# When the attention's parts run: one block per four chain steps, or evenly over the first 56 of 64

## The chip, the cores and the metric

The kernel runs on one core of a Trainium2 chip. The metric is the device time of one execution in microseconds (us). The kernel before took 3438.3 us (median of three runs, 3437.28 to 3444.45).

## The reference, cut to what matters

One encoder layer over 2048 tokens of width 1024. After a normalisation, one projection gives the inputs of two token mixers and their gates. A router then sends tokens to 16 experts of a SwiGLU block, which is more than half of the time but is not touched here.

```
u = rms_norm(x) @ w_in
# mixer 1, RWKV-7: state S (64x64 per head, 8 heads), one scan forward, one in reverse
S = S*w_t - (S@kk_t)(a_t*kk_t)' + v_t k_t' ;  y_t = S @ r_t
y_rwkv = (layer_norm(y_forward + y_reverse)*ln_w + ln_b + bonus) * g
# mixer 2, attention in a window of 128 tokens to each side: 16 blocks of 128 queries
y_attn = softmax(q k' + alibi, sink) v
merged = sigmoid(g1)*(y_rwkv @ w_pr) + sigmoid(g2)*(y_attn @ w_pa)
x = x + merged @ w_out ;  x = x + moe(rms_norm(x)) ;  out = rms_norm(x)
```

## The kernel before

The program has these stages: the projections; a preparation of the scans; the chains (in `token_mixers`, from about 970 to 1760 us); the merge of the mixers (`stage3`); the experts (`stage4`).

**The chains.** Each scan is cut into 64 chunks of 32 tokens. A step s works on chunk s of the forward scan and on chunk 63-s of the reverse scan. In a step, and for each scan, TensorE multiplies (L654), ScalarE copies (`ur`, L658), TensorE multiplies (L661), ScalarE copies four quarters into the tile `W` (L666), TensorE multiplies (L672) and VectorE writes the new state into the `W` of the next step (L675). Each waits for the one before it. The eight small matmuls of L679 read the same `W` and give the step's output `y`; the chain does not wait for them at once. Four steps make a group, and a group fills one `y` tile in PSUM for each scan. There is one such tile per scan (`ps_y`, one buffer).

**What ties the groups together.** A `W` tile (`W_8640` and `W_8641` of the forward scan, `W_8662` and `W_8663` of the other) serves two steps, and there are two per scan. So the `W` of a group's first two steps is loaded anew for the first two steps of the next group: four DMAs of 32 KB on the SP queue (L622, issued with one for `PRA`, L611), which wait until the L679 of the old group have read it. From the second half on (group 8 and later) VectorE adds `y` to the stored half of the other scan (`yacc`, L841, two buffers). That frees the `y` tile for the next group. Then `finish_rwkv` runs twice per group, once for each of two token blocks: layer norm on VectorE, four transposes on TensorE (L705) into a `pa` tile, `yt` on ScalarE (L709, four activations), L711 and L712 on VectorE, and a DMA of `yt` to `yr` (L713). `yt` and its second input `bgl` (L689) have one buffer each:

```
yt = k.ln.tile([128, NPAIR, 128], F32, name="yt")      # pool k.ln has bufs=1
k.ps_a = es.enter_context(tc.tile_pool(name="ps_a", bufs=3, space=PSUM))
```

**Work beside the chains.** `gates.run(7)` puts 7 matmuls (L495) of the remaining projections behind each scan's step. The attention is a generator per block of 128 queries: loads; scores of 8 heads (L748 and L749, each pair followed by L751 on VectorE) in four parts; transposes (L780) and products with the values (L787) in the rest. A middle block has 8 parts, the first and last have 7, so there are 126. `pieces` runs the next parts, 3, 2, 4 and 0 of them behind the four steps of a group, and stops at a block's end: one block per group, the last behind step 62.

**What sets the order.** The program is handed to a scheduler, which orders each engine's instructions by a simulated timeline. Instructions of the chain have priority as if written 1200 instructions earlier, those of `finish_rwkv` 500; all others go by their place in the program. Buffers of a pool are taken in the order of the program: the `pa` tile of a `finish_rwkv` is one of three that the attention's parts before it in the program use too, so its transposes stand behind those parts. `stage3` begins with the matmuls of L86 to L88 into `pm`; its PSUM tiles lie where those of the chains were.

Of the kernel before, what the change touches and what calls it, by code (L numbers as in the profile page):

```python
# [21 lines left out]
NQ = 4  # L22
QT = T // NQ
NBLK = T // 128
# [25 lines left out]
GATE_FIRST, GATE_MID = 24, 40  # L50
GATE_PREP, GATE_STEP = 5, 7
QKV = 20, 19, 15, 16, 17, 18
PIECES = 3, 2, 4, 0
LEAD = 1200


# [478 lines left out]
def mixers(k):  # L535
    nc, tc = k.nc, k.tc
    with ExitStack() as es:
# [37 lines left out]
        k.inv = es.enter_context(tc.tile_pool(name="inv", bufs=1))  # L575
        k.gc = k.inv.tile([128, 2, NPAIR, T // C], F32, name="gc")
        token_mixers(k, gates, el)


# [266 lines left out]
def token_mixers(k, gates, el):  # L846
# [4 lines left out]
    with ExitStack() as es:  # L851
# [96 lines left out]
        def invert(n):  # L948
            if late:
                late[0].run(n)  # L950
                if late[0].i > C:
                    late.pop(0)
# [11 lines left out]
            nc.vector.tensor_copy(k.abias[:, i], t)  # L964
        att = [attention(k, b) for b in range(NBLK)]

        def pieces(n):
            for _ in range(n):
                if att:
                    gates.need(min(NQ - 1, (NBLK - len(att) + 1) // 4))  # L970
                if att and next(att[0], 0) == 0:
                    att.pop(0)
                    break

        def between(mark):
            gates.run(GATE_STEP, after=mark)

        gates.run(GATE_MID)
        for s in range(NSTEP):
            run.step(s, between)  # L980
            pieces(PIECES[s % 4])
            invert(4)
        while att:
            pieces(9)
        while gates.todo:
            gates.run(24)

# [550 lines left out]
```

## Time and profile before

| | us |
|---|---|
| median of three runs | 3438.3 |
| the profiled execution's own time | 3432.75 |
| span of the profile, first to last instruction | 3430.9 |
| last TensorE instruction of the chains, end | 1761.1 |
| first TensorE instruction of `stage3` | 1805.4 |

The profile names engines PE (TensorE matmul), PEld (its weight load), DVE (VectorE), ACT (ScalarE), POOL (GpSimd) and SP (the queue that issues most DMAs). L495 is line 495 of the kernel. A row of a timeline has start, duration, engine, line, operation, tiles, and, in brackets, the idle time before it and what ended that. One row of L654, L661, L672 or L679 in the order below is two matmuls in the trace (x8 there, x16 here), and so is one of L787.

### The profile page before, as it was taken

To read this page: it belongs to the slowest core of one execution; us is meant where nothing else is said; L and a number is where in the kernel's file an instruction comes from. 1 tells how busy PE (TensorE), PEld (TensorE's weight loads), DVE (VectorE), ACT (ScalarE), POOL (GpSimd) and SP (SyncE) were. 2 spreads that over 40 slices of the span, in tenths; PEclk is the share of its full clock that TensorE was granted. 3 is DMA by queue.
4 is the path that set the end of the run, shared out by engine and by line. 5 is a ranking of instruction groups with operands and counts; after the bars stand their busy time and mean duration, and the time that the engine had idled before them with its cause. 6 is when DMAs were issued, how large, how long until landed. Compare 5 with 4: busy or idle time off the path is not lost. (4 is left out here: it accounts for less than half of the span.)

```text
span 3430.9 us, 65672 instructions
## 1 busy us (share of the span) xinstructions
PE 3170.0 (92%) x26062; PEld 2603.2 (76%) x26062; DVE 2321.3 (68%) x4902; ACT 1470.2 (43%) x2828; POOL 285.5 (8%) x457
## 2 busy tenths in 40 slices
PE   7999898889779998999969999659999999999998
PEld 6888676677556655666647888559999999999997
DVE  6434679898968889666776666466666666666665
ACT  5111455545424545455553333314444444444443
POOL 0000000000021111001000000001111111121111
PEclk9999899999989999999989999879999999999999
DMA  4212587868787777577666554336666666666663
GB/s 145 85 74 89 173 244 226 247 203 253 207 205 191 171 185 168 145 195 186 176 179 222 195 198 168 147 119 242 217 236 236 247 244 224 231 244 243 237 232 124
DMA packets 464579, 665.19 MB, mean 194 GB/s; under 512 B 162312, under 2 KB 345480, under 8 KB 445968
## 3 DMA queue, kind: packets, MB, share of 16 engines
q1 hardware_dynamic: 387824, 535.14, 50.5%
q10 hardware_dynamic: 58304, 59.79, 5.3%
q0 software_dynamic: 18144, 66.07, 5.1%
q8 instruction: 206, 3.38, 0.4%
q14 instruction: 101, 0.83, 0.1%
HBM read 483.66 MB, written 177.21 MB: 193 GB/s over the span
## 5 line engine op out<-in xcount | busy, mean ns | idle before, releaser
L495 PE MATMUL mm<-h,w 128*128 128x512 f32 x2112 | 602.1, 419 | 28.7 <-ACT ev L519 7.5
L86 PE MATMUL pg<-xs,wg 128*128 128x256 f32 x2048 | 583.6, 285 | 0.0
L87 PE MATMUL pg<-xs,wg 128*128 128x256 f32 x2048 | 582.0, 284 | 0.0
L88 PE MATMUL pg<-xs,wg 128*128 128x256 f32 x2048 | 579.6, 283 | 0.0
L495 PEld LDWEIGHTS mm<-h,w 128*128 128x128 f32 x2112 | 383.2, 194 | 123.0 <-DVE w L93 9.8
L87 PEld LDWEIGHTS pg<-xs,wg 128*128 128x128 f32 x2048 | 392.4, 192 | 4.6 <-DVE xs L1244 0.2
L86 PEld LDWEIGHTS pg<-xs,wg 128*128 128x128 f32 x2048 | 392.3, 192 | 4.6 <-ACT xs L1243 0.2
L88 PEld LDWEIGHTS pg<-xs,wg 128*128 128x128 f32 x2048 | 392.4, 192 | 0.0
L93 DVE TENSOR_TENSOR wg<-raw,wg 128x2048 fp32r<-128x2048 f32 x125 | 286.3, 2291 | 106.4 <-ACT wg L92 106.2
L92 ACT ACTIVATE w<-wraw 128x1024 fp32r<-128x1024 f32 x135 | 142.6, 1058 | 309.4 <-issue 155.2
L1331 ACT ACTIVATE sg<-pg 128x256 f32<-128x256 f32 x128 | 49.3, 385 | 488.4 <-PE pg L88 460.0
L92 ACT ACTIVATE wg<-raw 128x2048 fp32r<-128x2048 f32 x125 | 238.7, 1910 | 0.0
L405 DVE TENSOR_TENSOR tmp<-X,N 128x1 f32<-128x1 f32 (+30 forms) x248 | 188.4, 760 | 37.9 <-DMA N<-pra 17.6
L78 PE MATMUL mm<-h,w 128*128 128x512 f32 x480 | 190.0, 397 | 18.5 <-ACT w L92 12.8
L87 PE MATMUL py<-wd,hd 128*128 128x512 f32 x512 | 203.1, 397 | 0.0
L86 PE MATMUL py<-wd,hd 128*128 128x512 f32 x512 | 201.0, 393 | 0.0
L666 ACT ACTIVATE W<-ps 32x128 f32<-32x128 f32 x512 | 137.5, 269 | 147.9 <-PE ps L661 125.3
L93 DVE TENSOR_TENSOR w<-wraw,w 128x1024 fp32r<-128x1024 f32 x135 | 164.8, 1222 | 50.4 <-ACT w L92 50.0
L88 PE MATMUL py<-wd,hd 128*128 128x512 f32 x512 | 198.4, 390 | 0.0
L79 PE MATMUL mm<-h,w 128*128 128x512 f32 x480 | 189.3, 395 | 0.0
L80 PE MATMUL mm<-h,w 128*128 128x512 f32 x480 | 188.8, 394 | 0.0
L1332 DVE TENSOR_TENSOR sg<-pg,sg 128x256 f32<-128x256 f32 x128 | 54.1, 423 | 192.6 <-ACT sg L1331 192.6
(302 smaller groups left out, 6374.0 us busy)
## 6 DMA issues: line engine op xcount, KB each, us to landing
raw<-w_exp SPq DMA_DIRECT2D x128, 1536.0 KB, 6.9
wraw<-w_in SPq DMA_DIRECT2D x103, 512.0 KB, 5.1
PRA<-pra SPq DMA_DIRECT2D x64, 512.0 KB, 5.2
pra<-PR SPq DMA_DIRECT2D x64, 256.0 KB, 4.0
pra<-A SPq DMA_DIRECT2D x64, 256.0 KB, 3.8
kt<-KT ACTq DMA_DIRECT2D x128, 128.0 KB, 5.0
gl<-ev ACTq DMA_DIRECT2D x64, 256.0 KB, 4.2
KT<-kt SPq DMA_DIRECT2D x128, 128.0 KB, 5.3
```

What stands on the lines that cost most here:

```text
L78: nc.tensor.matmul(ps, lhsT=w[:, 0, i], rhs=hs[i][:, 0], start=(i == 0), stop=False)
L79: nc.tensor.matmul(ps, lhsT=w[:, 0, i], rhs=hs[i][:, 1], start=False, stop=False)
L80: nc.tensor.matmul(ps, lhsT=w[:, 1, i], rhs=hs[i][:, 0], start=False, stop=(i == KD - 1))
L86: nc.tensor.matmul(out, lhsT=w[0], rhs=x[0], start=start, stop=False)
L87: nc.tensor.matmul(out, lhsT=w[0], rhs=x[1], start=False, stop=False)
L88: return nc.tensor.matmul(out, lhsT=w[1], rhs=x[0], start=False, stop=stop)
L92: nc.scalar.activation(hi, x, AF.Copy)
L93: (eng or nc.vector).tensor_sub(lo, x, hi)
L405: nc.vector.tensor_mul(tmp[:, :i, :i], X[:, r, r], col[:, None, :].to_broadcast([128, i, i]))
L495: nc.tensor.matmul(self.ps, lhsT=w[:, t // 2, i], rhs=h[:, t % 2], start=(self.i == 0), stop=(self.i == 3 * KD - 1))
L666: nc.scalar.activation(W[qd(u), o, e].rearrange("p g i -> p (g i)"), ps[qd(u), 128:256], AF.Copy)
L1332: nc.vector.tensor_mul(sg, pg[:, 1], sg)
```

## The change

`pieces` with its table of numbers is replaced. Behind step s, parts run while fewer than (128/56)(s+1) have run, so two or three behind each step; the 126th stands behind step 54, and behind the last nine steps stands none. No instruction is added or removed, and the wait for the projections of later token quarters (`gates.need`) is called as before.

```diff
-PIECES = 3, 2, 4, 0
+ATT_END = 56
...
-        def pieces(n):
-            for _ in range(n):
-                if att:
-                    gates.need(min(NQ - 1, (NBLK - len(att) + 1) // 4))
-                if att and next(att[0], 0) == 0:
-                    att.pop(0)
-                    break
+        def piece():
+            gates.need(min(NQ - 1, (NBLK - len(att) + 1) // 4))
+            if next(att[0], 0) == 0:
+                att.pop(0)
...
+        parts = 0
         for s in range(NSTEP):
             run.step(s, between)
-            pieces(PIECES[s % 4])
+            while att and parts * ATT_END < 8 * NBLK * (s + 1):
+                piece()
+                parts += 1
             invert(4)
         while att:
-            pieces(9)
+            piece()
```

What the scheduler makes of it differs from step 26 on. The first place is TensorE at the boundary between group 12 (steps 48 to 51) and group 13. Before, around step 49, the forward scan's L679 on `W_8640` stood between the chain's own matmuls:

```order
L679 MATMUL y_16874<-W_8640,PRA_16498 32x64
L654 MATMUL ps_17110<-W_8662,PRA_16567 32x64 x8
L679 MATMUL y_16874<-W_8640,PRA_16498 32x64 x3
L495 MATMUL mm<-h,w 128x512 x7
L679 MATMUL y_16874<-W_8640,PRA_16498 32x64
L672 MATMUL ps_17060<-W_8640,KT_8644 64x64 x8
L679 MATMUL y_16874<-W_8640,PRA_16498 32x64 x3
```

(`y_16874` and below `y_17136` and `y_17137` are the `y` tiles of group 12; a number on `W_` or `ps_` names one buffer.) The next L654 on `W_8640`, of step 52, stood 52 rows further. Now all 64 L679 of the group stand at its end, and that L654 is the row behind them:

```order
L679 MATMUL y_17136<-W_8640,PRA_16740 32x64 x16
L679 MATMUL y_17136<-W_8641,PRA_17142 32x64 x9
L705 MATMUL pa<-ident,yacc 128x128 x4
L748 MATMUL pa<-kh,qs 128x384
L749 MATMUL pa<-kl,qs 128x384
L679 MATMUL y_17136<-W_8641,PRA_17142 32x64 x5
L748 MATMUL pa<-kh,qs 128x384
L749 MATMUL pa<-kl,qs 128x384
L679 MATMUL y_17136<-W_8641,PRA_17142 32x64 x2
L679 MATMUL y_17137<-W_8662,PRA_16809 32x64 x16
L679 MATMUL y_17137<-W_8663,PRA_17202 32x64 x16
L654 MATMUL ps_17855<-W_8640,PRA_17449 32x64 x8
```

The L679 moved from the steps that compute their `W` to the end of the group; the same holds at the ends of groups 10, 11, 13, 14 and 15.

The second place is TensorE at the end of the chains. Before, eight score pairs (L748, L749) of the last attention block stood behind the last chain matmuls, and behind those came its transposes and products, two `finish_rwkv` and `stage3`:

```order
L780 MATMUL pa<-ident,sc 128x128 x5
L787 MATMUL pa<-pT,vs 64x512
L780 MATMUL pa<-ident,sc 128x128 x11
L705 MATMUL pa<-ident,yacc 128x128 x4
L787 MATMUL pa<-pT,vs 64x512 x2
L705 MATMUL pa<-ident,yacc 128x128 x4
L787 MATMUL pa<-pT,vs 64x512
L86 MATMUL pm<-ysp,w 128x512
```

Now the row of the last chain matmuls (L661) is followed by this:

```order
L661 MATMUL ps_19408<-ur_19417,X 32x64 x8
L705 MATMUL pa<-ident,yacc 128x128 x4
L787 MATMUL pa<-pT,vs 64x512 x2
L705 MATMUL pa<-ident,yacc 128x128 x4
L787 MATMUL pa<-pT,vs 64x512
L679 MATMUL y_19062<-W_8640,PRA_18755 32x64 x16
L679 MATMUL y_19062<-W_8641,PRA_19068 32x64 x16
L679 MATMUL y_19063<-W_8662,PRA_18815 32x64 x16
L679 MATMUL y_19063<-W_8663,PRA_19128 32x64 x16
L705 MATMUL pa<-ident,yacc 128x128 x16
L86 MATMUL pm<-ysp,w 128x512
```

The last block's scores and transposes moved ahead of the chain's end, and behind it now stand six `finish_rwkv` (four L705 each: those of groups 13, 14 and 15) where two stood.

## Rows read from the trace of the kernel before

**Rows 1.** Busy us (and instructions) of each engine by stretch, then PE clock, DMA share, GB/s.
```profile
1280.00:1400.00 120.00, 103.48 (x1491) 68.24 (x1490) 108.20 (x234) 55.09 (x169) 13.30 (x42) 0.91 0.69 175
...
1600.00:1700.00 100.00, 99.78 (x1302) 65.37 (x1301) 72.19 (x223) 58.37 (x174) 9.84 (x32) 1.00 0.67 181
1700.00:1760.00 60.00, 57.85 (x793) 35.68 (x792) 39.64 (x122) 32.90 (x103) 2.44 (x8) 1.00 0.57 150
1761.00:1805.00 44.00, 14.13 (x53) 7.60 (x48) 29.29 (x90) 21.61 (x49) 0.00 (x0) 0.65 0.66 210
```

**Rows 2.** The same view, of L658 alone: two of them make a step.
```profile
1500.00:1600.00 100.00, 4.48 (x17) 0.98 0.75 196
```

**Rows 3.** Timeline of PE at the end of the chains.
```profile
1758.61 0.42 PE L661 MATMUL ps<-ur,X 32*32 32x64 f32 x16
1759.88 1.19 PE L679 MATMUL y<-W,PRA 128*32 128x64 f32 x16 [0.84 <-ACT W L666]
...
1763.29 0.36 PE L748 MATMUL pa<-kh,qs 128*128 128x256 f32 x1 [2.23 <-DVE qs L737]
...
1795.17 0.66 PE L705 MATMUL pa<-ident,yacc 128*128 128x128 f32 x4
1795.76 1.07 PE L787 MATMUL pa<-pT,vs 128*64 128x512 f32 x2
1805.43 0.79 PE L86 MATMUL pm<-ysp,w 128*128 128x512 f32 x1 [8.59 <-ACT yt L709]
```

**Rows 4.** Timeline of ACT at the end of the chains.
```profile
1755.83 1.46 ACT L709 ACTIVATE yt<-pa,vec 128x128 f32<-128x128 f32 x4
...
1759.55 1.15 ACT L666 ACTIVATE W<-ps 32x128 f32<-32x128 f32 x4 [0.60 <-PE ps L661]
...
1765.82 1.50 ACT L709 ACTIVATE yt<-pa,vec 128x128 f32<-128x128 f32 x4 [1.28 <-DMA yr<-yt]
...
1794.27 1.50 ACT L709 ACTIVATE yt<-pa,vec 128x128 f32<-128x128 f32 x4 [1.97 <-PE pa L705]
...
1803.87 1.50 ACT L709 ACTIVATE yt<-pa,vec 128x128 f32<-128x128 f32 x4 [6.40 <-DMA yr<-yt]
```

**Rows 5.** Timeline of PE within a step; the next row's start ends a row's share.
```profile
1632.33 0.43 PE L679 MATMUL y<-W,PRA 128*32 128x64 f32 x16
1632.69 0.69 PE L672 MATMUL ps<-W,KT 128*64 128x64 f32 x16
...
1633.76 0.34 PE L748 MATMUL pa<-kh,qs 128*128 128x384 f32 x1
1633.94 0.33 PE L749 MATMUL pa<-kl,qs 128*128 128x384 f32 x1
...
1634.56 1.91 PE L495 MATMUL mm<-h,w 128*128 128x512 f32 x7
```

**Rows 6.** Who waited for L625 (clearing in `W`), 1400 to 1760 us: us, times.
```profile
PEld ps L654: 0.7, 2
```

**Rows 7.** Timeline of SP: a reload of `W`; the DMAs of a finish.
```profile
1645.13 2.13 SPq L622 DMA_DIRECT2D W<-vtok  x4
...
1797.26 0.57 SPq L689 DMA_DIRECT2D bgl<-bg  x1
1797.88 0.66 SPq L713 DMA_DIRECT2D yr<-yt  x1
```

**Rows 8.** Issue to landing, 1400 us on: `W` (L622), then `yr` (L713).
```profile
DMA to landing us min/median/max: 1.6/3.8/6.8
...
DMA to landing us min/median/max: 2.6/3.9/7.2
```

**Rows 9.** Timeline of DVE behind the L709 of 1794.27.
```profile
1795.81 0.69 DVE L711 TENSOR_TENSOR yt<-yt,bgl 128x512 f32<-128x512 f32 x1 [1.09 <-ACT yt L709]
1796.54 0.69 DVE L712 TENSOR_TENSOR yt<-yt,bgl 128x512 f32<-128x512 f32 x1
```

**Rows 10.** The page's first line.
```profile
span 3430.9 us, 65672 instructions
```

## The prediction, made blind

> **What bounds the kernel now.** I read the stretches first, then the timelines around the chains' end. From 1600 to 1760 us TensorE is busy 99.8 of 100 and 57.9 of 60 us, and no other engine is near that [rows 1]: the reader is to see that late chain steps, at 17 L658 in 100 us some 11.8 us each [rows 2], last as long as TensorE's work in them. From 1280 to 1400 us VectorE is busy 108.2 of 120 us and TensorE 103.5, so neither has much room there [rows 1]. Then comes a hole: from 1761 to 1805 us TensorE works 14.1 of 44 us at a mean granted clock of 0.65, between its two levels, [rows 1]. The last chain matmuls start at 1758.61, the last L679 ends at 1761.07, the last attention block starts at 1763.29, and the merge starts at 1805.43, 8.59 us late because of ACT's L709 [rows 3]. The reader is to see that this L709 is the fourth in a series. Each writes the one `yt` tile, and two of the three gaps end on the landing of `yr<-yt`: 1755.83 to 1765.82 is 9.99 us, 1794.27 to 1803.87 is 9.60 us; between them lie 28.45 us [rows 4]. From the end of the last L666 (1759.55+1.15 = 1760.70) to 1805.43 the hole is 44.7 us [rows 3, 4].
>
> So there are two prices: TensorE's stalls up to the chains' end, and the length of the hole behind it. The experts and the merge keep their instructions, and their order is nearly the same, so what the chains lose or gain reaches the end unchanged.
>
> **The change part by part.** The table asks for an end nine steps earlier. The order gives less: late attention stands about one block ahead of before, and the last block's scores stand in steps 61 and 62. What moves more is the output work. The transposes of a `finish_rwkv` take a `pa` tile, and behind step 4g+3 there are now more attention parts before them in the program (for g = 13 all 16 blocks instead of 14). So they come later, `yacc` comes later, the `y` tile is freed later, and the 64 L679 of a group gather at its end.
>
> *TensorE's work up to the chains' end.* Out of the stretch behind the last L661 go 8 score pairs, 16 L780 and one L787; into it come 56 L679 and four more finishes' L705. A score pair of 384 columns takes 1633.94-1633.76+0.17, about 0.35 us, and these have 256, so at most 2.8 us for 8; sixteen transposes like the four of 0.66 us take 2.6; one L787 1.07 [rows 3, 5]. Sixteen L679 in the trace (8 in the order) take 1632.69-1632.33 = 0.36 us, so 56 take 2.5; four times 0.66 are 2.6 [rows 3, 5]. Moved ahead of the chains' end: 6.5-5.1 = about +1 us (0 to 2), since TensorE there has no room.
>
> *The reload of `W` at a group's boundary.* In the trace it lies far ahead of its use: from 1400 to 1760 us L654 waited twice, 0.7 us in all, for the clearing of the rest of `W` behind the same L679 [rows 6]. Now the L654 of step 52 stands right behind the L679 that free its tile. From the release: five issues (four `W` in 2.13 us [rows 7], `PRA` ahead or between), the last some 2.1 us after; landing 3.8 us later (1.6 to 6.8) [rows 8]: 5.9 us (3.7 to 8.9). What covers it is TensorE's own rows between: 48 L679 2.2 us, four L705 0.66, two score pairs 0.7: 3.5 us. The stall is 2.4 us (0.2 to 5.4). By the same count the boundary behind group 11 has 3.6 us of cover, those behind 13 and 14 some 5, with seven L495 at 1.9 us [rows 5] in the former, and that behind group 10 6.6. Together 2.4+2.3+0.9+0.9+0 = 6.5 us (0 to 21). I add 1.5 us because at two of them L705, `yacc` and L679 now follow each other with little between (0.7 us of VectorE each, as L711 [rows 9]): 8 us. I take the median landing because the row of 1645.13 is such a load in the same stretch. Everything behind that L654 on TensorE, gates and attention too, waits with it, as the queue is in order.
>
> The Trainium skill ("DMA: Bandwidth & Descriptors", section "Rules for kernel authors") says to issue a DMA early and wait for it late, which speaks against this order; its section "Anatomy of one DMA" gives some 2.0 us fixed for one on the GpSimd path. With that in place of the median landing of 3.8 us, an estimate from the page, the first two boundaries would cost 1.3 us, the others nothing, and my sum would fall by some 5 us. These DMAs go out on SP, and here the trace is above the page.
>
> *One block more before step 40.* It goes where VectorE has 11.8 us free in 120 and TensorE 16.5 [rows 1]. If the holes take it, up to 6 us are won back; if VectorE is late for the chain by it, as much is lost. Nothing in the rows decides; I take 0 (-6 to +6).
>
> *The hole behind the chains.* Before, three cycles of `yt` lay in it, but attention and the layer norm of the last group on VectorE put 28.45 us between the second and third L709 [rows 4]. Now the first L709 (group 13) stands behind the last L666 on ACT, and five more follow; `stage3` stands behind all. A cycle: L709, L711, L712 (1.5+0.7+0.7), the issues of `bgl` and `yr`, together 3.61 us from the start of L709 to the issue at 1797.88 [rows 4, 7, 9], and a landing of 3.9 us (2.6 to 7.2) [rows 8]: 7.5 us (6.2 to 10.8). The two cycles at this very place were 9.60 and 9.99 us [rows 4], with the merge's loads beside them, and those loads stay. I take 9.8. Layer norms of groups 14 and 15 run inside these cycles, as do the splits for the merge. Five cycles and the last L709: 5*9.8+1.5 = 50.5 us against 44.7, +5.8 us (32.5-44.7 = -12 by the shortest landing, +11 by the longest; more if VectorE stalls as before).
>
> *Sum.* +1 +8 +0 +6 = +15 us. The profiled execution took 3432.75 us (span 3430.9 [rows 10] and 1.85 around it), so it would take 3448; the median of the runs before is 3438.3, so 3453 us.
>
> **The rivals.**
>
> *Faster: the hole shrinks as the table intends.* Attention leaves VectorE and ACT behind the chains' end, so nothing stretches the series. If `yr` lands in 3 us, a cycle is 6.6 us and the hole 34.5: -10; with +1 and boundaries that stay covered (2 us), and 4 us won before step 40, -11: 3427 us. For it: the shortest landings of both kinds [rows 8], and VectorE's load in the hole falls. Against it: the two cycles at this place, and a DMA share of 0.66 there [rows 1]. It decides where a cycle is under 8.6 us, since 5*8.6+1.5 = 44.5.
>
> *No change.* A cycle at the median landing, 7.5 us, gives a hole of 39 us, -5.7; +1 and +8: +3, 3441 us. For it: the median is of 16 such DMAs. Against it: in the middle of the chains the queue is less full.
>
> *Much slower: boundaries at their longest.* If the loads land after 6.8 us and the second scan's reload, five issues behind the first, is late too, five boundaries cost 21 us; with a series stretched once by 8 us through VectorE's wait for the merge's weights: +1+21+6+8 = +36: 3474 us. For it: 28.45 us between two L709 [rows 4] shows that such stretching happens. Against it: no attention is left to stretch it.
>
> *The change does little at all,* since the scheduler undoes most of it: by the order it does, for attention, but not for L679 and L705; its price would be that of "no change".
>
> **How the numbers follow.** My forecast (+3 to +28 us, 3441 to 3466) 0.50; faster 0.16; no change, with the scheduler's undoing, 0.18; much slower 0.16. 0.2% is 7 us, about what a measurement of this kernel can tell from no change. Slower by more than that: the last case and most of the forecast, 0.62; within it: no change and the forecast's low end, 0.20; faster: 0.18. The range reaches down to 3432, inside the faster case, and up to 3474, leaving about 0.1 on each side.
>
> **What would show it.** In the profile after: L654 with idle time put down to `W` (POOL's L625, or a DMA) once per group from step 44 on, 1 to 5 us each, where none was; L679 in runs of 64 and more; behind the last L666 six L709, five of them ended by `yr<-yt`, 9 to 10 us apart; the first `pm` matmul 48 to 53 us behind the last L666. TensorE's work in the hole falls from 14 us to about 10. The forecast is wrong if the L709 are under 8 us apart, or if TensorE has no gaps at the boundaries because the load lands within its cover; then the kernel is at or below its old time.

## The result, and the profile after

The changed kernel takes 3460.8 us (median of 8 runs, 3449.3 to 3464.7) against 3437.8 us for the kernel before beside it: a ratio of 1.0062, 95% interval 1.0051 to 1.0073, 23 us slower. The profiled execution of after took 3464.7 us, 3.9 above its median, and that of before 3432.75, 5 below, so the two traces lie 32 us apart: 9 of these come from which executions were profiled, and the terms below are those of the two traces. (Ratios and intervals in this document are worked out from all runs, so they are not the quotients of the medians.) The page's first line of after, for [rows 10]:

```profile
span 3462.9 us, 65637 instructions
```

PE, DVE, ACT and POOL have as many instructions on this page as on that of before (26062, 4902, 2828 and 457).

To place the 32 us I cut both traces where the same work has been done: at the first L658 of steps 24 and 44, at the end of the last L666, and at the first `pm` L86. (At step 40 the two kernels are level, 1466.0 and 1466.1 us, but after had run 62 L495 fewer since step 24; by step 44 both have run 279.) Worked out from the starts of L658, L666 and L86:

| stretch | before, us | after, us | difference |
|---|---|---|---|
| span's start to step 24 | 1253.5 | 1256.2 | +2.7 |
| steps 24 to 43 | 267.2 | 274.9 | +7.7 |
| step 44 to the end of the last L666 | 240.0 | 255.0 | +15.0 |
| hole: last L666 to first `pm` | 44.7 | 50.95 | +6.2 |
| first `pm` to the span's end | 1625.5 | 1625.8 | +0.3 |

The stretches of after (columns as in [rows 1]): steps 24 to 43, step 44 to the last L666, the stretch of the second row of [rows 1], and the hole.

```profile
1256.20:1531.10 274.90, 246.58 (x3189) 164.20 (x3189) 201.62 (x455) 127.82 (x370) 25.41 (x82) 0.93 0.61 159
1531.10:1786.10 255.00, 224.52 (x2980) 147.41 (x2978) 165.76 (x511) 134.99 (x406) 20.66 (x68) 0.93 0.64 167
...
1600.00:1700.00 100.00, 88.26 (x1189) 58.76 (x1190) 66.56 (x198) 50.83 (x145) 9.72 (x32) 0.93 0.62 157
...
1787.00:1836.00 49.00, 7.38 (x147) 4.89 (x146) 34.83 (x97) 19.96 (x38) 0.00 (x0) 0.57 0.82 269
```

And the first two stretches in the trace of before:

```profile
1253.50:1520.70 267.20, 246.34 (x3160) 164.40 (x3161) 202.75 (x475) 128.49 (x374) 25.84 (x82) 0.95 0.65 169
1520.70:1760.70 240.00, 233.35 (x3108) 151.73 (x3106) 166.82 (x499) 132.59 (x396) 20.86 (x68) 0.99 0.68 180
```

From 1600 to 1700 us, where before had TensorE busy 99.78 of 100 us [rows 1], it now stands 11.7 us. From step 44 to the last L666 it idles 30.5 us against 6.7. The waits of TensorE's matmuls in this stretch of after are 30.0 us, and these are the eight largest of eleven rows (who waited, for whom: us in all, times, longest us):

```profile
PE ps L672 <- ACT W L666: 7.0, 8, 1.4
PE ps L654 <- DMA W<-vtok: 4.2, 2, 3.1
PE pa L780 <- DVE sc L772: 3.8, 3, 3.2
PE pa L748 <- DVE qs L737: 3.7, 1, 3.7
PE ps L654 <- DVE W L675: 3.2, 3, 1.8
PE ps L654 <- DMA PRA<-pra: 3.1, 2, 2.0
PE pa L787 <- DMA vs<-va: 2.1, 1, 2.1
PE y L679 <- DVE yacc L841: 1.0, 1, 1.0
...
```

The same view of before has four rows in all, 6.0 us:

```profile
PE ps L661 <- ACT ur L658: 2.1, 3, 1.5
PE y L679 <- ACT W L666: 1.7, 2, 0.8
PE mm L495 <- ACT ev L519: 1.5, 2, 1.2
PE ps L654 <- DVE W L675: 0.7, 1, 0.7
```

The reader is to see two kinds of new waits. L654 waits for a reload (`W`, `PRA`): 7.3 us in 4. And the chain's own latency lies bare: L672 waits for L666 eight times, since the L679 that stood between them have gone to the end of the group. The gather and the largest L654 wait of after, on PE's timeline, at the boundary behind group 12:

```profile
1624.23 0.97 PE L679 MATMUL y<-W,PRA 128*32 128x64 f32 x50
...
1628.23 1.10 PE L679 MATMUL y<-W,PRA 128*32 128x64 f32 x64 [0.96 <-DVE yacc L841]
1632.47 1.23 PE L654 MATMUL ps<-W,PRA 128*32 128x64 f32 x16 [3.14 <-DMA W<-vtok]
```

The 64 L679 of the second scan wait there for L841, which frees their `y` tile late. From step 44 to the last L666 the longest run of L679 with no other TensorE row in it is 18 in before and 74 in after. The landing of `W` in after, for [rows 8], has hardly changed:

```profile
DMA to landing us min/median/max: 1.6/3.7/6.1
```

Behind the last L666, ACT's timeline shows the six L709, for [rows 4]:

```profile
1786.04 1.46 ACT L709 ACTIVATE yt<-pa,vec 128x128 f32<-128x128 f32 x4
1796.12 1.50 ACT L709 ACTIVATE yt<-pa,vec 128x128 f32<-128x128 f32 x4 [3.70 <-DMA yr<-yt]
1808.33 1.50 ACT L709 ACTIVATE yt<-pa,vec 128x128 f32<-128x128 f32 x4 [0.21 <-DMA yr<-yt]
1819.59 1.50 ACT L709 ACTIVATE yt<-pa,vec 128x128 f32<-128x128 f32 x4 [2.16 <-DMA yr<-yt]
1825.95 1.50 ACT L709 ACTIVATE yt<-pa,vec 128x128 f32<-128x128 f32 x4 [1.77 <-DMA yr<-yt]
1835.54 1.50 ACT L709 ACTIVATE yt<-pa,vec 128x128 f32<-128x128 f32 x4 [8.08 <-DMA yr<-yt]
```

Five end on `yr<-yt`, but two of the waits are short (0.21 and 1.77). The waits of TensorE in the same hole point to a second series, the layer norms on VectorE (L702 is the last step of each):

```profile
PE pa L705 <- DVE yacc L702: 38.0, 4, 12.8
PE pm L86 <- ACT yt L709: 4.7, 1, 4.7
```

### The profile page after: what moved, and what is told of

Read it like the earlier page. It is cut to its first block, busy times and chain, and to the rows that moved or that the text cites. A ratio compares the mean times of both kernels' runs of the same rounds, so it can differ in the third digit from the quotient of the medians.

```text
span 3462.9 us, 65637 instructions
## 1 busy us (share of the span) xinstructions
PE 3159.6 (91%) x26062; PEld 2601.1 (75%) x26062; DVE 2326.4 (67%) x4902; ACT 1471.5 (42%) x2828; POOL 285.7 (8%) x457
## 5 line engine op out<-in xcount | busy, mean ns | idle before, releaser
L495 PE MATMUL mm<-h,w 128*128 128x512 f32 x2112 | 602.4, 420 | 26.5 <-DVE h L93 7.8
L86 PE MATMUL pg<-xs,wg 128*128 128x256 f32 x2048 | 583.8, 285 | 0.0
L495 PEld LDWEIGHTS mm<-h,w 128*128 128x128 f32 x2112 | 385.6, 195 | 120.1 <-DVE h L93 9.8
L86 PEld LDWEIGHTS pg<-xs,wg 128*128 128x128 f32 x2048 | 392.1, 192 | 4.6 <-ACT xs L1243 0.2
L86 PE MATMUL py<-wd,hd 128*128 128x512 f32 x512 | 200.9, 392 | 0.0
L666 ACT ACTIVATE W<-ps 32x128 f32<-32x128 f32 x512 | 137.1, 268 | 146.0 <-PE ps L661 127.2
```

What stands on the lines that cost most here:

```text
L86: nc.tensor.matmul(out, lhsT=w[0], rhs=x[0], start=start, stop=False)
L495: nc.tensor.matmul(self.ps, lhsT=w[:, t // 2, i], rhs=h[:, t % 2], start=(self.i == 0), stop=(self.i == 3 * KD - 1))
L666: nc.scalar.activation(W[qd(u), o, e].rearrange("p g i -> p (g i)"), ps[qd(u), 128:256], AF.Copy)
```

## The experiments

Theory A: an early attention makes the `finish_rwkv` late; they hold the two `yacc`, these hold the `y` tiles, so the L679 gather at the end of a group, and from that come both the late reloads and the bare chain. "Idle" in the table is TensorE's idle time from 1500 us to the last L666, in stretches over 300 ns; in the text, where a row of a window is shown, it is the window's length less PE's busy time.

| kernel | edit | idle | last L666 | hole | median us | ratio [95%] |
|---|---|---|---|---|---|---|
| before | | 5.9 | 1760.7 | 44.7 | 3437.8 | 1 |
| after | | 29.3 | 1786.1 | 51.0 | 3460.8 | 1.0062 [1.0051, 1.0073] |
| e1 | after, four `yacc` | 7.6 | 1757.8 | 81.2 | 3466.0 | 1.0074 [1.0059, 1.0089] |
| e2 | after, two `yt` | 27.3 | 1779.0 | 42.6 | 3452.3 | 1.0039 [1.0026, 1.0052] |
| e3 | after, even to step 64 | 6.5 | 1745.7 | 51.6 | 3429.2 | 0.9975 [0.9963, 0.9986] |
| e4 | after, finish's transposes apart | 6.0 | 1767.3 | 103.8 | 3495.7 | 1.0159 [1.0143, 1.0175] |
| e5 | before, two blocks earlier | 27.2 | 1805.1 | 28.4 | 3454.4 | 1.0039 [1.0022, 1.0055] |
| e6 | after, even to step 60 | 13.1 | 1762.6 | 54.3 | 3446.5 | 1.0023 [1.0011, 1.0035] |
| e7 | even to 64, two `yt` | 9.9 | 1758.4 | 36.8 | 3428.1 | 0.9968 [0.9956, 0.9979] |
| e8 | before, two `yt` | 6.5 | 1772.7 | 35.7 | 3434.2 | 0.9987 [0.9976, 0.9998] |
| f1 | after, two `yt`, three `yacc` | 14.1 | 1766.4 | 39.6 | 3437.3 | 1.0003 [0.9993, 1.0014] |
| f2 | e7, finishes pulled earlier | 5.0 | 1752.0 | 38.9 | 3416.5 | 0.9944 [0.9928, 0.9959] |

**e1: four `yacc`.**

```
-        self.yp = es.enter_context(tc.tile_pool(name="yp", bufs=2))
+        self.yp = es.enter_context(tc.tile_pool(name="yp", bufs=4))
```

> The changed kernel with four yacc buffers instead of two (pool yp). Theory A (late finish_rwkv hold yacc, so the y tile stays taken, the L679 gather at the group's end and the reload of W lands on the chain): by the order the L679 of groups 10 to 14 stand spread again, so TensorE's gaps between 1500 us and the chains' end, 29 us in the changed kernel, fall under 12, and the last L666 ends at 1760 to 1770 instead of 1786. Seven finishes now stand behind it, so the hole grows from 51 to 65 to 72 us. Sum: 5 to 12 us faster than the changed kernel, ratio to the kernel before 1.002 to 1.005. Rival B (the gaps come from the attention's own loads and VectorE work, packed into fewer steps): the gaps stay over 22 us, the last L666 stays at about 1785, the hole still grows, ratio 1.009 to 1.012.

With room for late finishes most of the stalls are gone. The longest run of L679 falls from 74 to 52, and from step 44 up to step 58 none is over 24. The waits of PE from step 44 to the last L666 (same columns), where after had 7.0 us for L672 and 7.3 for reloads:

```profile
PE pa L780 <- DVE sc L772: 2.4, 2, 1.2
PE ps L654 <- POOL W L625: 1.6, 3, 0.6
...
PE ps L672 <- ACT W L666: 0.5, 1, 0.5
```

```profile
1530.50:1757.80 227.30, 218.87 (x2975) 143.43 (x2973) 148.44 (x445) 124.07 (x377) 20.99 (x68) 0.98 0.67 173
```

The last L666 comes 28.3 us earlier, and 22 us of that are idle time in this stretch (30.5 to 8.4): theory A holds for the stalls. But the finishes are as late as ever: seven L709 stand behind the last L666, one more than in after, and the last block of attention stands there too, with 29.8 us between the first two L709. So the hole grew to 81.2 us, past the 65 to 72 expected, and the ratio missed its range: instead of 5 to 12 us faster than after, e1 is 5 us slower. PE's last wait in the hole:

```profile
1839.05 0.80 PE L86 MATMUL pm<-ysp,w 128*128 128x512 f32 x1 [23.45 <-ACT yt L709]
```

The Trainium skill ("Perfetto Trace Analysis", section "Optimization Strategy") says that gaps which repeat on the engine that should be full can mean too little room for the next tile, in number of buffers for one. For this stretch the trace agrees (29.3 to 7.6 us of idle with four buffers for two); the time of the kernel did not fall with it (1.0062 to 1.0074), because the wait moved.

**e2: two `yt`.**

```
-    yt = k.ln.tile([128, NPAIR, 128], F32, name="yt")
+    yt = k.ln.tile([128, NPAIR, 128], F32, name="yt", bufs=2)
```

> The changed kernel with two yt buffers instead of one. Theory A (the hole is a series of yt cycles ended by the landing of yr): the chains' end stays at 1780 to 1790, the L709 behind it no longer wait for yr, and the hole falls from 51 to 28 to 36 us; ratio 1.000 to 1.002. Rival C (the hole is as long as the layer norms on VectorE and the merge's loads make it): the hole stays at 45 to 51 us, ratio 1.005 to 1.006.

The hole fell by 8.4 us only, to 42.6, short of the 28 to 36 expected and below the rival's 45 to 51; the ratio, too, came out between the two. PE's waits in it say what is left:

```profile
PE pa L705 <- DVE yacc L702: 34.5, 4, 11.0
PE pm L86 <- ACT yt L709: 1.6, 1, 1.6
```

The wait for `yt` went from 4.7 to 1.6 us, the one for the layer norms from 38.0 to 34.5: two series ran side by side, and the second is nearly as long. The expectation took the first for the whole. The two `yacc` hold the layer norms back too: in the hole of e1, with four, TensorE's wait for L702 is short, and the series of `yt` is left (the 23.45 us above):

```profile
PE pa L705 <- DVE yacc L702: 8.8, 1, 8.8
```

Up to the chains' end e2 has the table and the gather of after (longest run 72) and nearly its idle time, 28.0 us from step 44 to the last L666. But this is made up otherwise:

```profile
1527.70:1779.00 251.30, 223.29 (x3016) 147.85 (x3005) 167.20 (x515) 134.23 (x406) 21.39 (x70) 0.94 0.65 170
```

```profile
PE ps L654 <- DMA W<-vtok: 7.6, 3, 6.1
...
PE ps L654 <- DMA PRA<-pra: 3.8, 3, 2.8
PE ps L672 <- ACT W L666: 3.7, 6, 1.7
```

So the idle time repeats with the gather, and its split between reloads (7.3 us in after, 11.4 here) and bare chain (7.0 and 3.7) does not.

**e3: the same table, even to step 64.**

```
-ATT_END = 56
+ATT_END = 64
```

> The changed kernel with ATT_END 64: the parts are spread evenly, two behind each step, but end as late as before. Theory A (the early end is what puts attention ahead of the finishes): no L679 gather, last L666 at 1757 to 1768, four L705 groups behind it, hole 43 to 50 us; ratio 0.998 to 1.002. Rival D (the even spreading itself is what costs, since each step then has a part): gaps over 20 us as in the changed kernel, ratio 1.005 to 1.007.

This is the cleanest cut between "even" and "early". The L679 stay spread (longest run 28), and from step 44 to the last L666 it takes 224.3 us against 240.0 before and 255.0 after, with 4.3 us idle (and 22.3 idle in steps 24 to 43, against 20.9 and 28.3):

```profile
1253.80:1521.40 267.60, 245.33 (x3131) 159.53 (x3131) 204.48 (x472) 127.23 (x372) 25.93 (x82) 0.94 0.65 168
1521.40:1745.70 224.30, 220.02 (x3087) 143.02 (x3085) 164.60 (x496) 130.79 (x391) 21.00 (x68) 0.99 0.74 189
```

Even parts gain; the early end costs more than that. Where they gain is open: of the 15.7 us that this stretch is shorter than before, only 2.4 are idle time (6.7 to 4.3), the rest is busy time of TensorE, part of it work that now stands in the hole. The last L666 came 11 us before the range expected, the hole was 1.6 us over its range and the ratio just under.

**e4: a PSUM buffer of their own for the finish's transposes.**

```
-    pt = k.ps_a.tile([128, 4, 128], F32, name="pa")
+    pt = k.ps_f.tile([128, 4, 128], F32, name="pf")
...
-        k.ps_a = es.enter_context(tc.tile_pool(name="ps_a", bufs=3, space=PSUM))
+        k.ps_a = es.enter_context(tc.tile_pool(name="ps_a", bufs=2, space=PSUM))
+        k.ps_f = es.enter_context(tc.tile_pool(name="ps_f", bufs=1, space=PSUM))
```

> The changed kernel with the transposes of finish_rwkv in a PSUM buffer of their own, and two instead of three pa buffers for the attention. Theory A (the shared pa buffers tie the finishes to the attention parts ahead of them): the L679 are spread, only two finishes stand behind the chains' end, and three attention blocks have fallen behind it; the chains end at 1735 to 1755, the hole is 55 to 75 us, ratio 0.998 to 1.006. Rival B (attention itself makes the gaps): gaps over 20 us before the chains' end in spite of spread L679, ratio over 1.008.

The finishes no longer queue behind attention for `pa`, and the idle up to the chains' end falls to 6.0 us, as theory A wants. But attention has one `pa` fewer and falls three blocks behind; the hole, its row here, holds 65.8 us of TensorE work where after has 7.4:

```profile
1768.00:1871.00 103.00, 65.81 (x172) 28.84 (x171) 54.69 (x168) 39.22 (x95) 0.00 (x0) 0.65 0.35 102
```

Chains' end, hole and ratio all missed what I expected. It fits the link from `pa` to the stalls and says nothing on the price. Nor does it prove the link by itself: its L495 came later too, 480 of them from step 44 to the last L666 where after has 256, and they are other work that TensorE could do beside the chain.

**e5: the uneven table of before, with two blocks moved ahead.**

```
             pieces(PIECES[s % 4])
+            if s in (15, 31):
+                pieces(9)
```

> The kernel before with its table (3, 2, 4, 0), and one whole block more behind steps 15 and 31: the attention ends early, as in the changed kernel, but block by block, not evenly. Theory A (the early end puts attention ahead of the finishes, the L679 gather, the reload of W stalls the chains): by the order the L679 of groups 10 to 13 gather, so gaps of 15 to 25 us between 1500 us and the chains' end, last L666 at 1770 to 1790; only two finishes and no attention stand behind it, so the hole falls from 44.7 to 25 to 36 us; ratio 1.000 to 1.006. Rival E (an early end costs nothing where it is not spread): gaps under 10 us, last L666 at 1755 to 1765, ratio 0.993 to 0.997.

An early end without even parts: 27.2 us of idle (a little over the 15 to 25 expected), L679 gathered in runs of up to 54, L672 waiting 5.6 us for L666, ratio 1.0039. The early end makes a loss without even parts, and by e3 even parts make none without the early end. The last L666 came at 1805, later than the 1770 to 1790 expected, and the hole was the shortest of all.

**e6: even to step 60.**

```
-ATT_END = 56
+ATT_END = 60
```

> The changed kernel with ATT_END 60, between 56 (slower) and 64 (faster). Theory A: by the order the L679 gather only in the last group, so gaps of 5 to 12 us, last L666 at 1745 to 1760, four finishes behind it and hole of 46 to 54 us; ratio 0.997 to 1.002, a threshold rather than a slope. Rival F (cost grows evenly with how early the end is): halfway between the two measured ratios, 1.002, with about half of the 29 us of gaps, 14 to 18.

1.0023 and 13.1 us: between the ends, and over the ranges that I expected for a threshold. The three ratios (64, 60, 56: 0.9975, 1.0023, 1.0062) lie near a line, as the rival has it. But what they are made of differs. In e6 the long runs of L679 come only at the end (60 behind step 62, before it none over 26), and in the stretch from step 44 on nothing waits for a reload and L672 for L666 only 0.2 us:

```profile
1530.80:1762.60 231.80, 217.86 (x3052) 142.53 (x3051) 159.34 (x464) 128.53 (x384) 20.57 (x68) 0.99 0.67 178
```

That stretch is shorter than before's 240.0. The trace of e6 loses its time ahead of it (step 44 starts at 1530.8, in before at 1520.7) and in the hole (54.3 against 44.7). So the gather behaves as a threshold, as theory A said, and the time does not follow it alone.

**e7 and e8: two `yt` with the even table to 64, and in the kernel before** (the edit of e2; e7 with that of e3).

> ATT_END 64 and two yt buffers: what the runs so far point to. Theory A: gaps stay under 10 us, last L666 at 1743 to 1753, hole 51.6 less the 8 us that two yt buffers saved in the changed kernel, so 41 to 46 us; ratio 0.994 to 0.997. Rival C (in this kernel the layer norms, the last attention block and the merge's loads set the hole): hole 48 to 54 us, ratio 0.997 to 0.999.

> The kernel before with two yt buffers. Theory A (in the kernel before, one long gap of 28 us came from VectorE's queue and only the last 6.4 us of waiting from yr): hole 38 to 43 us instead of 44.7, ratio 0.998 to 1.000. Rival C2 (the yt series sets the whole hole there too): hole under 34 us, ratio 0.996 or less.

In both the hole falls by 9 to 15 us, to below the range expected, and in both the profile shows the last L666 12 to 13 us later (in e7 past the 1743 to 1753 expected), so that the ratio moves by 0.0007 in e7 against e3, whose intervals overlap, and by 0.0013 in e8. The stretch from step 44 to the last L666, in e7 and then in e8, shows what makes the chains end later:

```profile
1522.70:1758.40 235.70, 226.99 (x3112) 147.82 (x3110) 168.78 (x503) 132.01 (x397) 20.66 (x68) 0.99 0.69 183
```

```profile
1522.20:1772.70 250.50, 244.19 (x3118) 157.91 (x3117) 168.92 (x513) 135.18 (x401) 20.66 (x68) 0.99 0.64 169
```

TensorE is busy 7.0 us longer than in e3 (220.02) and 10.8 longer than in before (233.35): rows of attention have moved into the stretch, from the hole (in e7 with two finishes) and in e8 also from before step 44. So part of what the hole loses in e7 is a shift and no gain. Besides, the profiled execution of e8 lies 4.7 us above its median and that of before 5 below its own.

**f1: two `yt` and three `yacc`** (the edits of e2 and e1, with 3 for 4), **and f2: e7 with the finishes pulled ahead.**

```
-                with tc.high_priority(offset=500):
+                with tc.high_priority(offset=1200):
                     finish_rwkv(k, blk[d], acc)
```

> Both buffers at once on the changed table: two yt, three yacc (four and two don't fit the memory). Theory A (the loss is the gathered L679 up to the chains' end; the series of yt behind it is the price of whatever is left over there): with three yacc the gather is only halved (groups of 28 to 36 L679 at a boundary instead of 64 and more), so the gaps of TensorE from 1500 us to the chains' end fall from 29 to about 12 to 18 us, the last L666 ends 1762 to 1775; six finishes stay behind it with two yt, so the hole is that of the two-yt kernel, 40 to 50 us instead of 51, ratio 0.998 to 1.002. Rival G (the gather only moves the stall: every microsecond won before the last L666 is lost behind it, as with four yacc alone): hole 60 to 75 us, ratio 1.004 to 1.008.

> The table evenly to step 64, two yt, and finish_rwkv's part pulled earlier by the scheduler (priority 1200 instead of 500); L679 are then spread nearly evenly (at most 24 in a step). Theory A: chains' end as in the 64-step kernels or 2 to 5 us earlier (1743 to 1758), the same hole, 35 to 45 us; ratio 0.995 to 0.998, not apart from the 64-step kernel with two yt (0.9968). Rival: finishes pulled ahead crowd VectorE and ScalarE in the chains' steps; chains' end later by 5 to 15 us, ratio 0.999 to 1.003.

f1 is level with before: one more `yacc` and one more `yt` give back the whole 23 us, half of the idle (29.3 to 14.1) and 11.4 us of the hole (51.0 to 39.6, a little under what was expected). So the two prices, the gathered L679 and the finishes behind the chains' end, cover most of the loss. Not all of it: the second `yt` helps the kernel before as well (e8, 0.9987), and f1 is 0.0016 behind that, with intervals that just overlap. f2 is the fastest here, 21 us under before. Its stretch from step 44 to the last L666:

```profile
1522.30:1752.00 229.70, 227.27 (x3123) 147.18 (x3122) 167.01 (x502) 135.37 (x401) 21.04 (x68) 1.00 0.71 186
```

With even parts and the finish early, TensorE idles 2.4 us in 230 and the hole is 38.9 us. Its ratio came out just under the range I gave; its interval and that of e7 (0.9956 to 0.9979) still touch, so the share of the earlier finishes in the gain is not sharp. The early end with finishes pulled ahead, step 56 and priority 1200, was not run; it would be the most direct test of theory A.

## Why the prediction was right in its direction, and which terms were mis-sized

*The hole, +5.8: right in size, half right in cause.* It measured +6.2 (50.95 us where 50.5 were worked out). Six L709 stand in it, five ended by `yr<-yt`, as said; TensorE works 7.4 us in it where about 10 were expected. The pace was less even than 9 to 10 us, 6.4 to 12.2, mean 9.9. That `yr` alone sets it was too simple: by e2 the layer norms are a second series of nearly the same length. The number came out so close because the cycle of 9.8 us was taken from two measured ones, whatever set them, and not from the landing (7.5 us); that is part luck.

*The reload, +8: right as what it names.* L654's waits on `W` and `PRA` by DMA are 7.3 us in 4, against 6.5 without the allowance; the longest is 3.14 where 2.4 (0.2 to 5.4) was worked out. Boundary by boundary it fits less well: behind groups 10 to 14 the waits are 1.96, 1.14, 3.14, 1.08 and none, where 0, 2.3, 2.4, 0.9 and 0.9 were worked out. And e2, with the same gather, has 11.4 us, so that the sum came out so near is luck in part. The rule cited in the prediction, to issue a DMA early and wait late (the Trainium skill, "DMA: Bandwidth & Descriptors", section "Rules for kernel authors"), is borne out by these waits and by e3, in which none of them is left from step 44 on.

*What else the gathered L679 cost: a mis-sized term.* The step "I add 1.5 us because at two of them L705, `yacc` and L679 now follow each other" was to cover everything but the reload. From step 44 on the waits rose from 6.0 to 30.0 us, by 24; the reload is 7.3 of it. The L679 were not only work to be done later: they were what TensorE did while ACT and VectorE answered. Without them L672 waits 7.0 us for L666, and single late answers (L780, L748, L787: 9.6 us) find nothing to stand in front of them. I priced what the moved rows wait for, and not what used to hide behind them. That it is the gather is shown by e1, which keeps the table and brings the idle to 7.6 us, and by e3, which undoes the gather in another way and brings it to 6.5. How the waits divide among the rows is that of one execution (e2).

*Work up to the chains' end, +1: it does not show as such.* PE's busy time from step 44 on fell by 8.8 us (233.35 to 224.52), so that of 24 us more waiting the stretch is 15.0 longer, where 9 were worked out (+1 and +8). The moved rows do not explain the fall: by their number in the stretch (6 score pairs and 12 L780 more, 12 L705 and 124 L679 fewer) and the prediction's own prices they come to about -1 us. The fall is in the small matmuls, L679 by 19.8 us, and L661 by 6.6 with as many of them, while L495 and attention grew. L679 alone, in after and in before, then L661 (the columns of PE and PEld only, then clock, DMA share, GB/s):

```profile
1531.10:1786.10 255.00, 12.18 (x522) 9.13 (x520) 0.93 0.64 167
```

```profile
1520.70:1760.70 240.00, 32.02 (x646) 17.20 (x646) 0.99 0.68 180
```

```profile
1531.10:1786.10 255.00, 17.17 (x640) 10.79 (x640) 0.93 0.64 167
```

```profile
1520.70:1760.70 240.00, 23.78 (x640) 13.28 (x640) 0.99 0.68 180
```

Of the L679, 124 fewer lie in the stretch, since the last group's stand behind the last L666. For the rest these sums mislead: the record of one small matmul lasts 0.22 us, longer than the 0.02 us or so to the next start in a run, and its end overlaps what follows. Many short runs have many such ends, which count as busy and may cover short waits. So how the 15.0 us divide into waits and work is not sharp; their sum is.

*One block more before step 40, 0 (-6 to +6): +7.7 over steps 24 to 43,* outside its bounds, and the largest single miss of the sum (the stretch from step 44 on missed by 6). The rows did not decide between a gain and a loss there, and 0 was taken; the block cost time: with as many L495 run, idle rose from 20.9 to 28.3 us. At step 40 itself it seemed nothing, since L495 had been put off. No experiment took it apart; e1, e2 and f1, with the same table, show +6.6, +8.2 and +3.7 there, and e3, which is one eighth slower, +0.4.

In sum, +15 was worked out; the traces differ by 32, of which 2.7 arose before step 24 (after, e1, e2 and f1, with one table, get there between 1251.0 and 1256.7 us, so as much is a matter of the execution), the medians by 23. By the traces the sum is short by 17, of which 6 lie in the stretch from step 44 on, 7.7 in the one before it and 2.7 ahead of that; by the medians it is short by 8, inside the range. In the first of these, two errors offset each other, a term left at 1.5 us for the bare chain and a fall of the busy time that was not worked out either; that is luck. Of the rivals, "faster" and "no change" fail on the L709's pace and on the idle; "much slower" came near the size of the chains' loss, but from the wrong cause, since the waits on reloads are 7.3 us and not 21; "does little" fails outright. None of the cases split the change into its two halves: evenness, which gains (e3), and the early end, which loses (e5, and e3 against after).

## What to carry to other kernels

Rows that the bounding engine can do at any time are cover, so before moving them count what waits beside them now, not only what they will wait for. Where a late consumer holds a buffer, follow the chain of buffers back (here `pa`, `yacc`, `y`, `W`) until it reaches the critical chain; more buffers stopped the stall here but left the late work behind (e1), so try to bring the consumer earlier instead, as in f2, the fastest run. And compare two traces where the same work is done, not at the same step.

## What the runs showed of the hardware that was not expected

What a line's busy time says of small matmuls depends on how they stand. One L679 has a record of 219 ns (median in both traces), yet a run of 64 takes 1.10 us (the row of 1628.23), 17 ns each, and one of 16 takes 0.43 [rows 5], 27 ns each. So the 12.18 us for 522 in after and the 32.02 us for 646 in before are 23 and 50 ns each without the matmul itself having become cheaper by so much: the ends of short runs overlap the rows behind them.

The clock was lower where the stalls were. In the stretch from step 44 on the granted clock, a mean over its two levels (1.2 and 2.4 GHz), is 0.93 in after and 0.99 in before, and the 256 L495, the same in number, take 76.15 us and 72.07:

```profile
1531.10:1786.10 255.00, 76.15 (x256) 47.57 (x256) 0.93 0.64 167
```

```profile
1520.70:1760.70 240.00, 72.07 (x256) 44.99 (x256) 0.99 0.68 180
```

In e3 and f2, with 4.3 and 2.4 us of idle, the clock is 0.99 and 1.00. The 4.1 us of these L495 are part of the 15.0 us, and no wait shows them.
